# A decoder step on one core: first tiles in halves, a lag on stored tiles, and the last norms paced anew

## The chip, the cores and the metric

The kernel runs on one core of one Trainium2 chip. The metric is the device time of one launch in microseconds. The profile is one such execution, recorded by the hardware; the other times are from executions without a profile.

TensorE (PE in the profile) does the matrix products, VectorE (DVE), ScalarE (ACT) and GpSimd (POOL) work on tiles in on-chip memory, and SyncE (SP) mostly issues transfers. Each engine works through its own instructions in order, and waits where one needs something that another engine or a transfer has not finished.

## The reference

One inference step of a small decoder with two layers, for a prompt of 1024 tokens and 8 decode tokens, all in float32, model width 2048. Cut to what matters here:

```python
def pool_layer(x, ...):                       # layer A
    u, gate = split(x @ w_in)                 # 2048 -> 2 x 2048
    d = multiscale_pool(u)                    # causal means over 2, 4, 8, 16 tokens, minus u
    d = einsum(d, w_grp) * scale              # four groups of 512 x 512
    return layer_norm(ALPHA * x + (d * silu(gate)) @ w_out)

k, v = shared_kv(h)                           # h: output of layer A; 4 heads of 64, rotary on 16

def attn_layer(h, ...):                       # layer B
    q, gate = split(h @ w_in)                 # 32 heads of 64, rotary on 16
    o = attn_core(q, k, v, window=128, sinks)
    return layer_norm(ALPHA * h + (o * silu(gate)) @ w_out)
```

Every layer ends with `layer_norm(ALPHA * x + sub(x))`: the mean and the variance are over the 2048 channels of a token. Outputs are y for prompt and decode tokens, the pooling states, and the last 128 keys and values.

## The kernel before

Channels lie on the 128 partitions, tokens along the free dimension. On-chip memory is cut into 53 slots of 128 x 1040 float32 (`Mem`, names m in the profile), handed out and returned as the work goes. The tokens are two chunks, c = 0 with 512 and c = 1 with 520 (the 8 decode tokens lie behind the prompt's). A pair of channel tiles for one chunk, 128 x (2 x 520), fills a slot.

**Phases.** Four large products follow each other (`PH`): `ai` (input x, weights in_wia), `ao` (input g, weights in_woa, with the residual and layer A's norm), `bi` (input h, weights in_wib and the shared K/V, with attention beside it), `bo` (input o, weights in_wob, the residual and layer B's norm). Each is cut into 2 x 2 blocks and computed with seven block products in place of eight; the seven (idx 0 to 6) run in three groups, A (0 and 5, of chunk 0 alone), C (1, 3, 6) and B (2, 4). For some of them the input is a sum or difference of blocks of both chunks; those are made by `t_ops` and stored in a scratch array (`Td`). `t_gen("x")` makes them for the kernel's input x, one channel pair at a step, with two loads, four VectorE operations and two stores each; the C group of `ai` is the first to read them.

**Units and ticks.** A unit is one block product for one output tile of 128 channels. Each float32 operand is split in two: ScalarE casts the raw tile to a rounded high part (weights L385, inputs L516), VectorE subtracts to get the low part (L393, L522). For each of eight channel tiles three matmuls follow, high x high, high x low, low x high (L589 to L591), so a unit has 24 matmuls of 512 columns in group A, or two halves of 24 matmuls of 260 columns (`HV`). A tick is 12 matmuls of 512 columns or 24 of 260; `self.i` counts ticks. At each one, `end()` issues what stands in a calendar (`on`, `at`, `product`), then the soft tasks that are due or for which a cost model of the engines (`calm`) sees room, then perhaps one step of the first side generator, then up to two loads of inputs (`x_tick`). Side generators (`t_gen`, `ln_gen`) are stepped at least every `every` ticks, provided that `room` slots are free; `pace(n)` sets `every`. The order in which PE, DVE and ACT work is the order in which this program issues instructions; the transfers on SP and GpSimd's work are ordered by a scheduler.

**Loads of inputs.** `x_tick` looks at the next twelve input tiles and issues up to two loads whose sources are written (`x_ready`, by a set `ok` of keys) and for which there is room; `far` is the number of ticks until the tile is read. The input tiles of `ao`, `bi` and `bo` are read back from arrays g, h, o that the kernel itself has written. A key goes into `ok` at the moment that the store is issued. `x_next` picks casts and subtractions of landed tiles; `x_get` forces what a unit needs.

**Start.** `start` issues the first weight tile (512 KB in one transfer), eight x tiles (520 KB each, with two more weights between), then three small arrays of constants: prm, cst, mki. Then come the first weight's split, the splits of four x tiles, the second weight's split, and a cast of a constant matrix, jr, out of cst (L1787). TensorE's first instruction reads the first weight and the first x tile.

**Norms.** Chunk 0 of each of the two norms (`ln_gen` with c = 0, called by `ln0`) runs as a side generator in the B group of `ao` and of `bo`: sums over channels by matmuls with jr, then for eight channel pairs p a subtraction of the mean and a multiplication by 1/sigma on VectorE (L917 to L919), two scalings with per-channel constants on ScalarE (`affine`, L905), and a store on SP (L906). For layer A the result is h, which the `bi` phase reads back (loads at L510); for layer B it is the output y0. Chunk 1 of layer B's norm, output y1, is the last of the kernel. It is done in two token halves of 260 (`HV`): the first half while the last products run (`tail_part` puts its steps on ticks), the second in `tail_end`, behind the last matmul. `tail_sums` (L1265) forms the channel sums by matmul, `tail_stats` copies the mean (L1277), squares it, forms the variance and calls `rstd`, which takes Abs_reciprocal_sqrt on ScalarE and refines it once with three operations (L843 to L845). `tail_norm1` is a subtraction and a multiplication (L1286, L1287), `tail_norm2` two scalings (L1295) and the store. Two of the eight pairs have `tail_norm1` on GpSimd in both halves:

```python
for p in (7, 3):
    self.at(3, lambda p=p: self.tail_norm1(p, h, nc.gpsimd))
for n, p in enumerate((4, 0, 5, 1, 6, 2)):
    self.at(3 + n, lambda p=p: self.tail_norm(p, h))
for n, p in ((6, 7), (8, 3)):
    self.at(n, lambda p=p: self.tail_norm2(p, h))
```

The bank that a product adds to can be seeded by a copy on ScalarE (L711); after a unit its sums are moved out by ScalarE (L615, L649, L658) or VectorE (L660). The attention score products (L1463) and their VectorE partner (L1526) are not touched by the change.

Of the kernel before, what the change touches and what calls it, by code (L numbers as in the profile page):

```python
# [72 lines left out]
X_LOAD, X_CAST, X_LOW, X_FAR, X_SPARE = 9, 4, 3, 22, 8  # L73

# [82 lines left out]
class Kern:  # L157
# [331 lines left out]
    def x_plan(self):  # L489
        self.xl = [(ph, i, j) for ph in PH for _, idxs in GROUPS for i in idxs for j in JS[ph]]  # L490
        self.xraw, self.xhi, self.X = {}, {}, {}
        self.ok = {("x", c, m) for c in range(2) for m in range(NK)}
# [10 lines left out]
    def x_ready(self, k):  # L503
        return all(z in self.ok for z in self.x_src(k)[0])
# [39 lines left out]
    def x_tick(self):  # L544
        free = lambda: len(self.mem.whole())
        n = 0
        for k in self.xl[:12]:
            far = self.x_at(k) - self.i
            if far > X_FAR or n > 1:
                break  # L550
            if self.x_ready(k) and (
                (len(self.xraw) < 4 and free() > X_SPARE + 2) or (far <= X_LOAD and free() > 3) or far <= X_LOAD - 4
            ):
                self.x_load(k)
                n += 1
# [218 lines left out]
    def t_ops(self, A, E, O, Eb, Ob, n, kp, cs=slice(0, TMAX)):  # L774
# [13 lines left out]
        if cs.stop == TMAX:  # L788
            self.ok.add(("t", n, kp))

    def t_gen(self, n):
# [11 lines left out]
        for kp in range(8):  # L803
# [5 lines left out]
            yield  # L809
# [40 lines left out]
    def ln_gen(self, c, pre, acc, gc, bc, out, name):  # L850
# [49 lines left out]
        def affine(p):  # L900
# [6 lines left out]
            if name is not None:  # L907
                self.ok |= {(name, c, 2 * p), (name, c, 2 * p + 1)}
# [88 lines left out]
    def group_unit(self, u):  # L997
# [9 lines left out]
        def post(jj, banks):  # L1007
# [14 lines left out]
            if c == 0:  # L1022
                nc.gpsimd.dma_start(self.act["g", 0][:, m0 : m0 + 2, :TP], t)
                self.ok |= {("g", 0, m0), ("g", 0, m0 + 1)}
# [3 lines left out]
            self.ok.add(("g", 1, m))  # L1028
# [186 lines left out]
    def tail_part(self, q, pos, m, cs):  # L1215
# [54 lines left out]
    def tail_stats(self, h):  # L1270
# [9 lines left out]
        self.rstd(v, r, qq)  # L1280

    def tail_norm1(self, p, h, eng=None):
        eng = eng or self.nc.vector
        b2 = lambda x: x[:, None, h].to_broadcast([P, 2, THM])
        t = self.tv(p)[:, :, h]
        eng.tensor_sub(t, t, b2(self.L["m"]))  # L1286
        eng.tensor_mul(t, t, b2(self.L["r"]))  # L1287
# [10 lines left out]
    def tail_norm(self, p, h):  # L1298
        self.tail_norm1(p, h)
        self.tail_norm2(p, h)  # L1300

    def tail_end(self):
        h = HV[1]
        self.tail_stats(h)
        for p in (2, 7):
            self.tail_norm1(p, h, self.nc.gpsimd)
        for p in (4, 0, 5, 2, 1, 6, 7, 3):
            if p in (2, 7):
                self.tail_norm2(p, h)
            else:  # L1310
                self.tail_norm(p, h)
# [136 lines left out]
    def attend(self, c, t, at):  # L1448
# [103 lines left out]
        def gate():  # L1552
# [7 lines left out]
            if c == 0:  # L1560
                nc.gpsimd.dma_start(self.act["o", 0][:, t, :TP], a.a[:, :TP])
                self.ok.add(("o", 0, t))
# [32 lines left out]
    def o_ok(self):  # L1595
        if self.dec_done:
            for kp in self.half_done:
                self.ok |= {("t", "o", kp), ("o", 1, 2 * kp + 1)}
# [173 lines left out]
    def start(self):  # L1772
        nc, io = self.nc, self.io
        es = [u.ent for u in self.units[:4]]
        es[0]["load"]()
        for n in range(8):
            self.x_load(self.xl[0])
            if n in (3, 5):
                es[n // 2]["load"]()
        nc.sync.dma_start(self.prm[:], io["prm"])  # L1780
        nc.sync.dma_start(self.cst[:], io["cst"])
        nc.sync.dma_start(self.mki[:], io["mki"])
        es[0]["low"]()
        for n in range(4):
            self.x_get(("ai", 0, n))
        es[1]["low"]()
        nc.scalar.copy(self.jr, self.cst[:, K_J : K_J + P])  # L1787
# [23 lines left out]
    def run(self):  # L1811
# [25 lines left out]
        self.on(0, lambda: self.side.append(self.t_gen("x")), 0)  # L1837
# [11 lines left out]
        self.on(f["bo", "B"], pace(2))  # L1849
# [153 lines left out]
```

## Time and profile before

| | before |
|---|---|
| median of 3 runs | 2351.46 us (2350.6 to 2351.57) |
| profiled execution, its own time | 2350.32 us |
| span of the profiled execution | 2348.5 us |
| granted TensorE clock, mean | 0.99 |
| TensorE busy | 2290.5 us, 98% of the span, 16998 matmuls |
| VectorE, ScalarE, GpSimd busy | 66%, 47%, 9% |
| transfers | 555.65 MB, mean 237 GB/s |

The span runs from the first to the last instruction. In rows of the trace the first number is the start in us, the second the busy time of the instruction (or of the group of them), x the number in the group; m is a slot, pD a bank of TensorE's results, and a bracket at the end tells how long the engine had been idle and what ended that. In rows of windows come the stretch, its length, then busy time with the number of instructions for PE, PE's weight loads, DVE, ACT, POOL, the granted clock, the busy share of the transfer engines and GB/s. In the list of waits: engine and operation, what ended the wait, us in total, how many, the longest.

### The profile page before, as it was taken

How to read it: one execution, taken by the hardware profiler on the slowest of the kernel's cores; microseconds unless marked ns; L12 is line 12 of the kernel's file. 1: busy time of each engine (PE TensorE's matmuls, PEld its weight loads, DVE VectorE, ACT ScalarE, POOL GpSimd, SP SyncE). 2: the span in 40 equal slices, each digit the busy share in tenths (PEclk: the TensorE clock that was granted, in tenths of full speed). 3: DMA queues.
4: the chain of work that ended last, by engine and by line, in shares of the span. 5: the costliest groups of instructions: out<-in, count | busy, mean ns of one | idle time of the engine just before them, and what ended most of it. 6: DMA issues, size and time to landing. Idle time of an engine off the chain costs nothing. (4 is left out here: it accounts for less than half of the span.)

```text
span 2348.5 us, 42019 instructions
## 1 busy us (share of the span) xinstructions
PE 2290.5 (98%) x16998; PEld 2132.3 (91%) x16998; DVE 1547.3 (66%) x1840; ACT 1100.6 (47%) x2281; POOL 208.6 (9%) x424
## 2 busy tenths in 40 slices
PE   8999999999999999999999999999999999999994
PEld 6888999999999899988777899999999997799994
DVE  6447756656676686676675866665556676697667
ACT  4334333344243432454665635454656666542455
POOL 1101001100101111000010110100000000111002
PEclk9999999999999999999999999999999999999997
DMA  9858667674748798887596776666644555898844
GB/s 389 289 184 291 212 214 246 222 245 131 265 149 326 241 342 275 299 280 246 166 341 217 250 237 215 213 217 209 214 143 150 165 183 202 273 373 290 281 135 145
DMA packets 194483, 555.65 MB, mean 237 GB/s; under 512 B 31088, under 2 KB 36080, under 8 KB 194288
## 3 DMA queue, kind: packets, MB, share of 16 engines
q1 hardware_dynamic: 152592, 402.42, 52.6%
q0 software_dynamic: 41696, 150.55, 16.4%
q8 instruction: 133, 2.18, 0.4%
q14 instruction: 62, 0.51, 0.1%
HBM read 372.04 MB, written 171.33 MB: 231 GB/s over the span
## 5 line engine op out<-in xcount | busy, mean ns | idle before, releaser
L589 PE MATMUL pD<-m,m 128*128 128x260 f32 (+1 forms) x4800 | 1459.7, 304 | 17.8 <-ACT m L516 7.9
L590 PE MATMUL pD<-m,m 128*128 128x260 f32 (+1 forms) x4800 | 1448.7, 302 | 0.8 <-DVE m L522 0.8
L591 PE MATMUL pD<-m,m 128*128 128x260 f32 (+1 forms) x4800 | 1447.9, 302 | 0.0
L589 PEld LDWEIGHTS pD<-m,m 128*128 128x128 f32 x4800 | 905.8, 189 | 70.7 <-issue 15.6
L590 PEld LDWEIGHTS pD<-m,m 128*128 128x128 f32 x4800 | 906.1, 189 | 36.2 <-DVE m L522 1.9
L591 PEld LDWEIGHTS pD<-m,m 128*128 128x128 f32 x4800 | 905.7, 189 | 35.9
L393 DVE TENSOR_TENSOR m<-m,m 128x1024 fp32r<-128x1024 f32 x366 | 445.0, 1219 | 185.5 <-ACT m L385 169.3
L385 ACT CAST m<-m 128x1024 fp32r<-128x1024 f32 x366 | 381.0, 1045 | 48.8 <-PE pD L590 13.4
L429 DVE TENSOR_TENSOR m<-m,m 128x1024 f32<-128x1024 f32 x200 | 243.8, 1219 | 19.6 <-PE pD L590 7.1
L649 ACT COPY m<-pD 128x260 f32<-128x260 f32 (+1 forms) x126 | 56.0, 445 | 324.3 <-PE pD L591 320.5
L522 DVE TENSOR_TENSOR m<-m,m 128x1040 fp32r<-128x1040 f32 x112 | 134.9, 1235 | 14.6 <-ACT m L516 14.3
L658 ACT ACTIVATE m<-pD 128x260 f32<-128x260 f32 x100 | 38.6, 386 | 202.2 <-PE pD L591 183.2
L516 ACT CAST m<-m 128x1040 fp32r<-128x1040 f32 x112 | 114.5, 1059 | 19.6 <-DVE m L393 6.5
L1526 DVE TENSOR_TENSOR m<-pS,cst 128x1024 f32<-128x1024 f32 x32 | 39.2, 1224 | 120.2 <-ACT m L1525 120.2
L660 DVE TENSOR_TENSOR m<-pD,m 128x260 f32<-128x260 f32 x100 | 42.6, 426 | 113.8 <-PE pD L591 106.4
L1499 ACT ACTIVATE m<-m,sm 128x128 f32<-128x128 f32 x256 | 99.3, 392 | 0.0
L615 ACT ACTIVATE m<-pD 128x512 f32<-128x512 f32 x50 | 29.9, 597 | 137.2 <-PE pD L591 122.7
L1048 PE MATMUL pD<-m,m 128*128 128x260 f32 (+1 forms) x576 | 91.3, 319 | 0.0
L1048 PEld LDWEIGHTS pD<-m,m 128*128 128x128 f32 x576 | 82.0, 188 | 8.2
L1512 ACT ACTIVATE m<-m,sm 128x128 f32<-128x128 f32 x256 | 81.6, 392 | 5.2 <-DVE sm L1507 5.0
L628 ACT ACTIVATE m<-pD 128x260 f32<-128x260 f32 x68 | 26.4, 388 | 117.1 <-PE pD L591 117.0
L630 ACT COPY m<-pD 128x260 f32<-128x260 f32 x68 | 25.6, 376 | 110.5 <-PE pD L591 110.5
(180 smaller groups left out, 1658.7 us busy)
## 6 DMA issues: line engine op xcount, KB each, us to landing
m<-in_wia SPq DMA_DIRECT2D x96, 512.0 KB, 5.3
m<-in_wib SPq DMA_DIRECT2D x96, 512.0 KB, 5.0
m<-in_woa SPq DMA_DIRECT2D x48, 512.0 KB, 6.1
m<-in_wob SPq DMA_DIRECT2D x48, 512.0 KB, 6.2
m<-in_x SPq DMA_DIRECT2D x36, 520.0 KB, 9.8
sbi<-m POOLq DMA_DIRECT2D x36, 512.0 KB, 3.9
m<-sbi SPq DMA_DIRECT2D x36, 512.0 KB, 4.5
sai<-m POOLq DMA_DIRECT2D x32, 512.0 KB, 4.1
```

The costliest lines, as they stand in the source:

```text
L385: self.nc.scalar.copy(e["hi"].r[:, :1024], e["raw"].a[:, :1024])
L393: self.nc.vector.tensor_sub(o.r[:, :1024], s.a[:, :1024], e["hi"].a[:, :1024])
L429: self.nc.vector.tensor_add(s[o].a[:, :1024], s[a].a[:, :1024], s[b].a[:, :1024])
L516: self.nc.scalar.copy(h.r[:, : 2 * TMAX], s.a[:, : 2 * TMAX])
L522: self.nc.vector.tensor_sub(o.r[:, : 2 * TMAX], s.a[:, : 2 * TMAX], h.a[:, : 2 * TMAX])
L589: nc.tensor.matmul(ps[:, :w], wh[:, s], h, start=new and n2 == 0, stop=False, skip_group_check=on)
L590: nc.tensor.matmul(ps[:, :w], wh[:, s], l, start=False, stop=False, skip_group_check=on)
L591: nc.tensor.matmul(ps[:, :w], wl[:, s], h, start=False, stop=n2 == 7, skip_group_check=on)
L649: self.evac(ph, pos)(self.dest(ph, pos, m, 0)(cs), ps[:, : cs.stop - cs.start])
L1048: nc.tensor.matmul(ps[:, : cs.stop - cs.start], ws[:, s], d[:, cs], start=f0 and k == 0, stop=l0 and k == 3,)
L1499: nc.scalar.activation(x["s3"][:, i, :], x["s3"][:, i, :], AF.Exp, bias=nm[:, i : i + 1], scale=0.125, accum_out=rs[:, i : i + 1],)
L1512: nc.scalar.activation(x["s3"][:, i, :], x["s3"][:, i, :], AF.Copy, scale=rs[:, i : i + 1])
```

## The change

It has three parts.

*The start.* The first weight tile and the first x tile are loaded in halves: weight half 0, the two halves of x tile 0, one more x tile, weight half 1, then the others, with the second weight where it was, the third one tile earlier, and the fourth among them too. Each half has a cast and a subtraction of its own. The constants are loaded behind the last x tile, cst first; the cast of jr (and a small VectorE operation on prm) is moved from the start to tick 8. `t_gen("x")` begins at tick 5 in place of 0 and leaves at least four ticks between two channel pairs.

*Loads behind a store.* `ok` keeps the tick at which a key was stored (`landed`). A load that reads g, h or o directly is issued only three ticks later than that (`X_LAG`), as long as its tile is over four ticks away from use (`X_URGE`). Loads from the scratch arrays of sums aren't held back.

*The last norms.* No pair of y1 is on GpSimd. In the first half the eight pairs stand at ticks 3, 4, 4, 5, 5, 6, 6, 7 behind the sums. In `tail_end`, the subtractions of the first two pairs (4 and 0) stand between the Abs_reciprocal_sqrt and the three refining operations, and the eight pairs are in the same order as before. For the side generator of y0's norm `every` is 1 from the start of the B group of `bo` and 2 from 13 ticks later; `room` is 1 from 12 ticks later.

```diff
--- before
+++ after
@@ -71,6 +71,7 @@
 L_LOAD, L_CAST, L_LOW = 11, 6, 4
 SLACK = 1.5
 X_LOAD, X_CAST, X_LOW, X_FAR, X_SPARE = 9, 4, 3, 22, 8
+X_LAG, X_URGE = 3, 4
 
 
 def in_order(tc):
...
@@ -489,7 +490,7 @@
     def x_plan(self):
         self.xl = [(ph, i, j) for ph in PH for _, idxs in GROUPS for i in idxs for j in JS[ph]]
         self.xraw, self.xhi, self.X = {}, {}, {}
-        self.ok = {("x", c, m) for c in range(2) for m in range(NK)}
+        self.ok = {("x", c, m): -99 for c in range(2) for m in range(NK)}
 
     def x_src(self, k):
         ph, i, j = k
...
@@ -500,8 +501,11 @@
         m = 4 * j + o
         return [(n, c, m), (n, c, m + 2)], self.act[n, c][:, m : m + 3 : 2, :]
 
-    def x_ready(self, k):
-        return all(z in self.ok for z in self.x_src(k)[0])
+    def landed(self, *keys):
+        self.ok.update((k, self.i) for k in keys)
+
+    def x_ready(self, k, lag=0):
+        return all(self.ok.get(z, 9999) + lag <= self.i for z in self.x_src(k)[0])
 
     def x_load(self, k):
         self.xl.remove(k)
...
@@ -548,7 +552,7 @@
             far = self.x_at(k) - self.i
             if far > X_FAR or n > 1:
                 break
-            if self.x_ready(k) and (
+            if self.x_ready(k, X_LAG if k[1] not in TROW and far > X_URGE else 0) and (
                 (len(self.xraw) < 4 and free() > X_SPARE + 2) or (far <= X_LOAD and free() > 3) or far <= X_LOAD - 4
             ):
                 self.x_load(k)
...
@@ -806,7 +810,9 @@
             av, bv = a.v(2, TMAX), b.v(2, TMAX)
             self.t_ops(a, av[:, 0], av[:, 1], bv[:, 0], bv[:, 1], n, kp)
             b.free()
-            yield
+            t = self.i + 4
+            while self.i < t:
+                yield
 
 
     def quiet(self):
...
@@ -836,10 +842,11 @@
             yield
         w.free()
 
-    def rstd(self, v, r, q):
+    def rstd(self, v, r, q, between=lambda: None):
 
         nc = self.nc
         nc.scalar.activation(r, v, AF.Abs_reciprocal_sqrt)
+        between()
         nc.vector.tensor_mul(q, r, r)
         nc.vector.scalar_tensor_tensor(q, q, -0.5, v, op0=ALU.mult, op1=ALU.mult)
         nc.vector.scalar_tensor_tensor(r, q, 1.5, r, op0=ALU.add, op1=ALU.mult)
...
@@ -905,7 +912,7 @@
                 nc.scalar.activation(t[:, j], t[:, j], AF.Identity, bias=b, scale=g)
             nc.sync.dma_start(out[:, 2 * p : 2 * p + 2, :T], t)
             if name is not None:
-                self.ok |= {(name, c, 2 * p), (name, c, 2 * p + 1)}
+                self.landed((name, c, 2 * p), (name, c, 2 * p + 1))
 
         for p in range(10):
             load(p + 2)
...
@@ -1244,12 +1251,8 @@
             return
         self.product(1, lambda: self.tail_sums(h, (0, 1), True, True), 1)
         self.at(2, lambda: self.tail_stats(h))
-        for p in (7, 3):
-            self.at(3, lambda p=p: self.tail_norm1(p, h, nc.gpsimd))
-        for n, p in enumerate((4, 0, 5, 1, 6, 2)):
-            self.at(3 + n, lambda p=p: self.tail_norm(p, h))
-        for n, p in ((6, 7), (8, 3)):
-            self.at(n, lambda p=p: self.tail_norm2(p, h))
+        for n, p in zip((3, 4, 4, 5, 5, 6, 6, 7), (4, 0, 5, 1, 6, 2, 7, 3)):
+            self.at(n, lambda p=p: self.tail_norm(p, h))
 
     def tail_sums(self, h, js, first, stop):
 
...
@@ -1277,38 +1280,29 @@
         nc.scalar.copy(m, mb[:, :THM])
         nc.vector.tensor_mul(qq, m, m)
         nc.vector.scalar_tensor_tensor(v, vb[:, :THM], EPS, qq, op0=ALU.add, op1=ALU.subtract)
-        self.rstd(v, r, qq)
-
-    def tail_norm1(self, p, h, eng=None):
-        eng = eng or self.nc.vector
-        b2 = lambda x: x[:, None, h].to_broadcast([P, 2, THM])
+        self.rstd(v, r, qq, between)
+
+    def tail_less(self, p, h):
         t = self.tv(p)[:, :, h]
-        eng.tensor_sub(t, t, b2(self.L["m"]))
-        eng.tensor_mul(t, t, b2(self.L["r"]))
-
-    def tail_norm2(self, p, h):
+        self.nc.vector.tensor_sub(t, t, self.L["m"][:, None, h].to_broadcast([P, 2, THM]))
+
+    def tail_norm(self, p, h, less=True):
         nc = self.nc
+        if less:
+            self.tail_less(p, h)
         t = self.tv(p)[:, :, h]
+        nc.vector.tensor_mul(t, t, self.L["r"][:, None, h].to_broadcast([P, 2, THM]))
         for j in range(2):
             m = 2 * p + j
             g, b = (self.prm[:, i + m : i + m + 1] for i in (C_GB, C_BB))
             nc.scalar.activation(t[:, j], t[:, j], AF.Identity, bias=b, scale=g)
         nc.sync.dma_start(self.io["y1"][:, 2 * p : 2 * p + 2, h], t)
 
-    def tail_norm(self, p, h):
-        self.tail_norm1(p, h)
-        self.tail_norm2(p, h)
-
     def tail_end(self):
         h = HV[1]
-        self.tail_stats(h)
-        for p in (2, 7):
-            self.tail_norm1(p, h, self.nc.gpsimd)
+        self.tail_stats(h, lambda: [self.tail_less(p, h) for p in (4, 0)])
         for p in (4, 0, 5, 2, 1, 6, 7, 3):
-            if p in (2, 7):
-                self.tail_norm2(p, h)
-            else:
-                self.tail_norm(p, h)
+            self.tail_norm(p, h, p not in (4, 0))
 
 
     def partner(self, s, n, T):
...
@@ -1772,22 +1766,49 @@
     def start(self):
         nc, io = self.nc, self.io
         es = [u.ent for u in self.units[:4]]
-        es[0]["load"]()
-        for n in range(8):
+        e, k = es[0], self.xl.pop(0)
+        raw, x = self.mem.full(), self.mem.full()
+        half = [slice(512 * i, 512 * i + 512) for i in range(2)]
+        xs = [slice(TMAX * i, TMAX * i + TMAX) for i in range(2)]
+        src = self.x_src(k)[1]
+        w = self.quads("ai", 0)[0]
+        nc.sync.dma_start(raw.a[:, half[0]], w[:, half[0]])
+        for i in range(2):
+            nc.sync.dma_start(x.a[:, xs[i]], src[:, i, :])
+        for n in range(7):
             self.x_load(self.xl[0])
-            if n in (3, 5):
-                es[n // 2]["load"]()
+            if n == 0:
+                nc.sync.dma_start(raw.a[:, half[1]], w[:, half[1]])
+            elif n in (2, 3, 5):
+                es[(n + 1) // 2]["load"]()
+        nc.sync.dma_start(self.cst[:], io["cst"])
         nc.sync.dma_start(self.prm[:], io["prm"])
-        nc.sync.dma_start(self.cst[:], io["cst"])
         nc.sync.dma_start(self.mki[:], io["mki"])
-        es[0]["low"]()
-        for n in range(4):
+        hi, lo, xh, xo = (self.mem.full() for _ in range(4))
+        def split(s, h, o, c):
+            nc.scalar.copy(h.r[:, c], s.a[:, c])
+            nc.vector.tensor_sub(o.r[:, c], s.a[:, c], h.a[:, c])
+
+        split(raw, hi, lo, half[0])
+        for i in range(2):
+            split(x, xh, xo, xs[i])
+        self.x_get(("ai", 0, 1))
+        split(raw, hi, lo, half[1])
+        e.update({"hi": hi, "lo": lo, "in": True, "did": {"cast", "low"}})
+        self.X[k] = xh, xo
+        for s in (raw, x):
+            s.free()
+        for n in range(2, 4):
             self.x_get(("ai", 0, n))
         es[1]["low"]()
-        nc.scalar.copy(self.jr, self.cst[:, K_J : K_J + P])
-        nc.vector.tensor_scalar(
-            self.nsink[:], self.prm[:, C_SINK : C_SINK + NH], -1.0, None, op0=ALU.mult
-        )
+
+        def consts():
+            nc.scalar.copy(self.jr, self.cst[:, K_J : K_J + P])
+            nc.vector.tensor_scalar(
+                self.nsink[:], self.prm[:, C_SINK : C_SINK + NH], -1.0, None, op0=ALU.mult
+            )
+
+        self.on(8, consts)
         z = self.mem.full()
         nc.gpsimd.memset(z.a[:, :144], 0.0)
 
...
@@ -1834,7 +1855,7 @@
         def ln1():
             self.side.append(self.ln_gen(1, {}, self.acc, C_GA, C_BA, self.act["h", 1], "h"))
 
-        self.on(0, lambda: self.side.append(self.t_gen("x")), 0)
+        self.on(5, lambda: self.side.append(self.t_gen("x")), 0)
         for g in range(2):
             t = f["ai", "B"] + 40 * g
             for k in (g, g + 2):
...
@@ -1846,7 +1867,9 @@
         self.on(f["bi", "A"], pace(2))
         self.on(f["bi", "A"] + 1, ln1)
         self.on(f["bo", "B"] + 3, lambda: ln0("bo", C_GB, C_BB, io["y0"], None))
-        self.on(f["bo", "B"], pace(2))
+        self.on(f["bo", "B"], pace(1))
+        self.on(f["bo", "B"] + 13, pace(2))
+        self.on(f["bo", "B"] + 12, lambda: setattr(self, "room", 1))
         self.on(f["bo", "B"], self.tail_open, 0)
         self.use_four(True)
         self.on(f["bi", "A"], lambda: self.use_four(False), 0)
```

The other hunks put `self.landed(...)` in the place of `self.ok.add(...)` and `self.ok |= {...}`, and an argument `between` through `tail_stats`.

More of the change, by code (lines that the diff above doesn't have):

```diff
@@ L788, in t_ops @@
         if cs.stop == TMAX:
-            self.ok.add(("t", n, kp))
+            self.landed(("t", n, kp))
     def t_gen(self, n):
@@ L1023, in post @@
                 nc.gpsimd.dma_start(self.act["g", 0][:, m0 : m0 + 2, :TP], t)
-                self.ok |= {("g", 0, m0), ("g", 0, m0 + 1)}
+                self.landed(("g", 0, m0), ("g", 0, m0 + 1))
                 G.free(True)
@@ L1027, in post @@
             nc.gpsimd.dma_start(self.act["g", 1][:, m, :], t[:, 1])
-            self.ok.add(("g", 1, m))
+            self.landed(("g", 1, m))
             def sums():
@@ L1268, in tail_sums, with tail_stats @@
                 )
-    def tail_stats(self, h):
+    def tail_stats(self, h, between=lambda: None):
         nc = self.nc
@@ L1561, in gate @@
                 nc.gpsimd.dma_start(self.act["o", 0][:, t, :TP], a.a[:, :TP])
-                self.ok.add(("o", 0, t))
+                self.landed(("o", 0, t))
                 self.ao.pop((c, t)).free(True)
@@ L1597, in o_ok @@
             for kp in self.half_done:
-                self.ok |= {("t", "o", kp), ("o", 1, 2 * kp + 1)}
+                self.landed(("t", "o", kp), ("o", 1, 2 * kp + 1))
     def gate_done(self, c, t0, s):
```

## The prediction

> **What bounds the kernel now.** I read the page first, then TensorE's own waits, then the order of time at the places that these name.
>
> ```profile
> span 2348.5 us, 42019 instructions
> ...
> PE 2290.5 (98%) x16998; PEld 2132.3 (91%) x16998; DVE 1547.3 (66%) x1840; ACT 1100.6 (47%) x2281; POOL 208.6 (9%) x424
> ```
> ```profile
> PE pS L1463 <- DVE m L1526: 8.8, 4, 3.9
> PE pD L589 <- ACT m L516: 7.9, 1, 7.9
> PE pD L589 <- ACT pD L711: 7.8, 3, 5.1
> PE pD L589 <- ACT m L658: 1.2, 1, 1.2
> ```
>
> TensorE is the bound: it is busy for 98% of the span, and the change leaves the number and the order of its matmuls as they are. So only three things can move the time: when the first matmul starts, the few stalls between, and what follows the last matmul. The waits list the stalls (us in total, times, longest). The first, 7.9, is the wait for the first tile; of the 7.8 behind L711, one wait of 5.1 is most. The 8.8 behind L1526 lie in attention, which the change does not touch.
>
> **The start.**
>
> ```profile
> 5.16 1.04 ACT L385 CAST m<-m 128x1024 fp32r<-128x1024 f32 x1 [3.14 <-DMA m<-in_wia]
> ...
> 6.76 1.06 ACT L516 CAST m<-m 128x1040 fp32r<-128x1040 f32 x1 [0.56 <-DMA m<-in_x]
> ...
> 7.85 5.31 DVE L522 TENSOR_TENSOR m<-m,m 128x1040 fp32r<-128x1040 f32 x4 [0.39 <-ACT m L516]
> 7.87 0.79 PE L589 MATMUL pD<-m,m 128*128 128x512 f32 x1 [7.87 <-ACT m L516]
> ...
> 10.82 1.06 ACT L516 CAST m<-m 128x1040 fp32r<-128x1040 f32 x1 [0.28 <-DMA m<-in_x]
> ...
> 13.15 0.63 PE L590 MATMUL pD<-m,m 128*128 128x512 f32 x1
> ...
> 13.58 0.50 PE L591 MATMUL pD<-m,m 128*128 128x512 f32 x1
> ...
> 13.92 0.39 PE L589 MATMUL pD<-m,m 128*128 128x512 f32 x1
> ...
> 16.69 0.40 PE L589 MATMUL pD<-m,m 128*128 128x512 f32 x1
> ...
> 19.68 0.30 ACT L1787 CAST jr<-cst 128x128 fp32r<-128x128 f32 x1 [6.54 <-DMA cst<-in_cst]
> ...
> 23.40 0.50 PE L589 MATMUL pD<-m,m 128*128 128x512 f32 x1 [0.97 <-ACT m L615]
> ```
> ```profile
> L982 ACT CAST m<-m 128x512 fp32r<-128x512 f32 x3 | 1.9, 620 | 0.9 <-DVE m L966 0.9
> ...
> L983 DVE TENSOR_TENSOR m<-m,m 128x512 fp32r<-128x512 f32 x3 | 2.1, 690 | 3.3 <-ACT m L982 3.3
> ```
>
> The weight tile lands at 5.16, the first x tile at 6.76, the fourth at 10.82: (10.82 - 6.76) / 3 = 1.35 us for each. The new order asks for the halves that the first matmul needs ahead of the rest. Half a tile takes about 0.67, so the first weight half lands at 5.16 - 0.67 = 4.5 and the first x half at 5.15; with a half cast of 0.62 the first matmul starts at 5.8 in place of 7.87. The splitting adds two casts and two subtractions of 0.62 and 0.69, which lie in time in which both engines waited for data (the idle time in the brackets).
>
> This doesn't carry through in full. The bytes ahead of the fourth x tile are the same, so it lands at 10.82 as before; the cast (1.06) and the subtraction (four in 5.31, ending at 13.16) make it whole at 13.15. The first unit has 24 matmuls, and the 20th is the first to read that low part: 13.15 + 5 x 0.23 = 14.3 is the earliest end. The other limit is the rate: 13.15 to 13.58 is one matmul per 0.43 us, 13.92 to 16.69 is twelve at 0.23, so TensorE ran at half rate from 7.87 to 13.6, 5.7 us. The same 5.7 after 5.8 is 11.5; twelve matmuls are done by then and twelve at 0.23 follow: 14.4. Before, the second unit began at 16.69. Gain 2.3. The Trainium skill (TensorE: Matmul & The Clock Gate, "What's actually happening") speaks against part of this: the rate is set by free-running windows of some 3.4 us, so an early start may only buy more matmuls at half rate. By it the gain here is an estimated 1.7 to 2.4; its late end is a rival below.
>
> The third unit began at 23.40, though 16.69 + 24 x 0.23 = 22.2. The brackets tell why: ScalarE sat for 6.54 until 19.68 before the cast of jr, which waits for the constants, and the weight and x casts and the eviction L615 stood behind it. The change moves that cast to tick 8 and issues the constants behind the last x tile; the x tiles and weights have then landed by 20.3 (six more at 1.35 behind 12.2), and nothing in the first units reads the constants. Gain 1.2. The transforms of x begin five ticks later, 14 us, and each takes at least four ticks; eight of them end long before the C group, 72 ticks in, so I cost this at nothing. Start: 3.5, bounds 1.5 (a half transfer that lands no sooner, and the jr gain) and 4.0.
>
> **The norm of h and its loads.**
>
> ```profile
> 1032.05 0.36 SPq L906 DMA_DIRECT2D h<-m  x1
> ...
> 1040.62 1.03 SPq L510 DMA_DIRECT2D m<-h  x2
> ...
> 1045.11 1.06 ACT L516 CAST m<-m 128x1040 fp32r<-128x1040 f32 x1 [5.73 <-DMA m<-h]
> ...
> 1049.29 0.59 PE L589 MATMUL pD<-m,m 128*128 128x260 f32 x1 [5.09 <-ACT pD L711]
> ```
> ```profile
> 2324.17 4.32 ACT L905 ACTIVATE m<-m,prm 128x512 f32<-128x512 f32 x6
> ```
> ```profile
> 1049.20:1054.90 5.70, 5.62 (x26) 5.62 (x27) 2.64 (x3) 2.72 (x6) 0.00 (x0) 0.50 0.90 321
> 1054.90:1060.60 5.70, 5.70 (x49) 5.70 (x49) 2.71 (x3) 5.37 (x8) 0.00 (x0) 1.00 0.96 346
> ```
>
> SP issues the store of h at 1032.05 and stands until 1040.62 before the load that reads it; the tile lands at 1045.11; ScalarE, in order, waits 5.73 with its cast; the copy into the accumulator (L711) stands behind, and TensorE waits 5.09. The third fence shows the aftermath: at a granted clock of 0.50, 26 matmuls in 5.70, and 49 in the next 5.70. So 26 x (5.70 / 26 - 5.70 / 49) = 2.7 are lost beside the 5.1: 7.8 are at stake.
>
> With the lag these loads are asked for three ticks after the store, and in the built order two more affine pairs stand ahead of the first pair of h casts. The load still waits for its store on SP, with later stores and a weight load behind it, and I see no reason for it to land before 1045.1. But ScalarE reaches that cast later: to the 1039.4 at which it ran dry come two affine pairs (the second fence has six of these affines, later in the run, at 0.72 each: 2.9) and two small copies, an estimated 1 with the handing over: 3.9, so some 1.8 of the wait is left. That is too little to halve the clock: the stretch quoted next has waits of 2.2 and 1.2 and a granted clock of 1.00. I take 7.8 - 1.8 = 6.0, bounds 2.0 (it waits nearly as long for the next pair) and 7.8.
>
> **The last stretch.**
>
> ```profile
> 2300.00:2322.00 22.00, 17.35 (x123) 15.45 (x122) 21.29 (x27) 13.11 (x25) 2.53 (x2) 1.00 0.46 165
> ```
> ```profile
> 2303.12 1.10 ACT L1295 ACTIVATE m<-m,prm 128x260 f32<-128x260 f32 x2 [5.35 <-DVE m L1287]
> ...
> 2305.95 0.39 PE L589 MATMUL pD<-m,m 128*128 128x260 f32 x1 [2.16 <-ACT pD L711]
> ...
> 2320.86 1.16 PE L1265 MATMUL pD<-m,cst 128*128 128x260 f32 x4 [0.93 <-DVE m L660]
> ...
> 2325.71 1.23 DVE L919 TENSOR_TENSOR m<-m,m 128x1024 f32<-128x1024 f32 x1
> ...
> 2328.40 0.35 ACT L1277 COPY m<-pD 128x260 f32<-128x260 f32 x1
> ...
> 2330.70 1.39 DVE L844 SCALAR_TENSOR_TENSOR m<-m 128x260 f32<-128x260 f32 x1
> ...
> 2332.12 0.43 DVE L845 SCALAR_TENSOR_TENSOR m<-m,m 128x260 f32<-128x260 f32 x1
> ...
> 2333.20 1.66 DVE L1287 TENSOR_TENSOR m<-m,m 128x520 f32<-128x520 f32 x1
> ...
> 2334.78 1.77 DVE L1286 TENSOR_TENSOR m<-m,m 128x520 f32<-128x520 f32 x1
> ...
> 2336.59 0.70 DVE L1287 TENSOR_TENSOR m<-m,m 128x520 f32<-128x520 f32 x1
> ...
> 2337.20 0.69 DVE L1286 TENSOR_TENSOR m<-m,m 128x520 f32<-128x520 f32 x1
> ...
> 2338.67 6.04 ACT L1295 ACTIVATE m<-m,prm 128x260 f32<-128x260 f32 x12 [0.25 <-DVE m L1287]
> ...
> 2341.97 0.70 DVE L1287 TENSOR_TENSOR m<-m,m 128x520 f32<-128x520 f32 x1
> ```
>
> VectorE is busy for 21.29 of 22.0, so ScalarE waits for it, and TensorE for ScalarE: 2.2 here and the 1.2 behind L658. The change takes three steps of y0's norm out of this stretch (two operations like L919's 1.23 each, 7.4 in all) and GpSimd's contention, and adds two tiles to VectorE ((2341.97 - 2336.59) / 4 = 1.35 each, 2.7): it falls to about 15. The seeding copy now stands ahead of most affines. The steps go to the time before 2300, where VectorE has room: the mean is 66%, a step is 2.45 in two ticks of 2.9. I take 2.5 of the 3.4, bounds 0 and 3.4.
>
> **Behind the last matmul** (the same fence). TensorE ends at 2320.86 + 1.16 = 2322.0, but the statistics start at 2328.40, behind the rest of y0's norm (the six affines from 2324.17, shown with h). In the changed program's order nothing of y0 stands there: they start at about 2322.1. Gain 6.3.
>
> From 2328.40 to the last affine (2338.67 + 6.04 = 2344.7) are 16.3. New count: copy, square and variance 1.3 (0.35, and 0.45 each by L845); two subtractions 1.4 (L1287's 0.70 each; in part of it VectorE waited for the root); three refining steps 1.3 at 0.43, since L844's 1.39 against L845's 0.43 goes with GpSimd; two multiplies 1.4 (L1286); six tiles at 1.35, 8.1; the last two affines 1.0 (6.04 / 12 each): 14.5. The two tiles that GpSimd had cost 2.7 more on VectorE, and 0.96 + 0.96 + 1.08 of stretched operations (L844, L1287, L1286) go. Gain 1.8; the last store and the end, 3.8, stay. Sum 8.1, bounds 7 and 8.6.
>
> **The rivals.** *The wait on h moves along:* the next pair, which needs stores that SP issues behind the waiting load, stalls instead. For it: SP's wait (1032.05 to 1040.62) stays in the order. The gain there is 2: 2335.4.
>
> *The clock keeps its own time:* half rate ends at an edge that does not move with the first matmul. The trace's one start, 5.7 us of it, can't tell. If the edge comes 1.1 later than forecast, at 12.6, (12.6 - 5.8) / 0.43 = 15.8 matmuls are begun, 15 are done, and the unit ends at 12.6 + 9 x 0.23 and a little: 15.0. That is 0.6 less: 2332.0. The Trainium skill's rule quoted with the start (TensorE: Matmul & The Clock Gate) is what would make the edge so, by its windows at an estimated 3.4 to 6.8 us behind the first matmul.
>
> *The end stays as it is:* the new pace doesn't finish y0's norm in time on the chip, and 6.3 and 2.5 go: 2340.2. Against it: the order is fixed at build time.
>
> *Slower: the lag starves the phases.* Every first-chunk load of g, h and o may come three ticks late, 3 x 2.9 = 8.7 (24 matmuls in 5.70 / 49 x 24 = 2.8 and a little); if TensorE waits for that at the start of three phases, 26 are lost and the 6 as well: 2363.4. It decides from 20 us of new waits. Against it: the lag is dropped within four ticks of need, and ScalarE's order differs at h alone. For it: the loads are issued in another order by SP throughout, and the trace of before can't show what that does.
>
> **How the numbers follow.** 3.5 + 6.0 + 2.5 + 8.1 = 20.1. The profiled execution took 2350.3 for its span of 2348.5 and becomes 2330.2; the runs' median, 1.1 above it, becomes 2331.4. Chances: forecast 0.62, wait moves 0.15, clock 0.08, end 0.04, slower 0.11. All upper bounds give 23.8, 2327.7, and the untouched attention stalls can go either way by a microsecond or two: 2326. All lower ones give 10.5, 2341.0; I stop at 2340, which leaves out the slower rival and the third at its worst. The gain can vanish only by the slower rival: of its 0.11 I give 0.02 to an end within 0.2% (4.7 us, about what a measurement can tell) and 0.09 to slower; faster is 0.89.
>
> **What would show it.** Right: first matmul near 5.8, third unit near 20; no TensorE wait over 2 and no clock of 0.50 around 1040; the copy of the mean within 0.3 of the last matmul, no GpSimd in the norm, 14.5 from there to the last affine. Wrong: an SP wait on h that still ends in a ScalarE wait of 4 or more; TensorE waits behind L715 or L662 from 2230 on; new waits for x casts at a phase's start.

## The result and the profile after

| | before | after |
|---|---|---|
| median | 2351.16 us (2350.6 to 2351.57) | 2325.91 us (2324.88 to 2327.5) |
| ratio, 95% interval | | 0.9893 (0.9876 to 0.9911) |
| profiled execution, its own time | 2350.32 us | 2326.44 us |
| its span, granted clock | 2348.5 us, 0.990 | 2324.5 us, 0.993 |

The changed kernel is faster by 25.2 us between the medians and by 23.9 between the two profiled executions, where 20.1 was forecast. The median lies 0.1 under the lower end of the range (2326.0). First the page of the changed kernel and TensorE's waits in it (us in total, times, longest); line numbers are up to 7 higher or 6 lower than before, outside of the new start.

```profile
PE 2286.2 (98%) x16998; PEld 2129.5 (92%) x16998; DVE 1546.7 (67%) x1850; ACT 1100.9 (47%) x2283; POOL 195.6 (8%) x416
```
```profile
PE pS L1457 <- DVE m L1520: 10.1, 5, 4.8
PE pD L593 <- ACT m L1789: 5.9, 1, 5.9
...
PE pD L594 <- DVE m L526: 0.6, 1, 0.6
PE pD L593 <- ACT pD L715: 0.6, 1, 0.6
```

Of 7.8 us behind the copy into the accumulator (L711, now L715) 0.6 is left, and the first wait is 5.9 in place of 7.9. Of the waits over 1 us only those in attention (L1463, now L1457) are no shorter: 4.8 at the longest against 3.9. The order of time, at the start:

```profile
4.54 1.93 ACT L1789 CAST m<-m 128x512 fp32r<-128x512 f32 x3 [2.53 <-DMA m<-in_wia]
...
5.87 0.80 PE L593 MATMUL pD<-m,m 128*128 128x512 f32 x1 [5.87 <-ACT m L1789]
...
11.99 0.50 PE L594 MATMUL pD<-m,m 128*128 128x512 f32 x1 [0.59 <-DVE m L526]
...
14.64 0.40 PE L593 MATMUL pD<-m,m 128*128 128x512 f32 x1
...
20.21 0.40 PE L593 MATMUL pD<-m,m 128*128 128x512 f32 x1
```

First matmul 5.87 (forecast 5.8), second unit 14.64 (14.4), third unit 20.21 (near 20). At the norm of h, ScalarE and then SP:

```profile
1033.91 1.53 ACT L912 ACTIVATE m<-m,prm 128x512 f32<-128x512 f32 x2 [1.11 <-DVE m L926]
...
1036.59 2.03 ACT L520 CAST m<-m 128x1040 fp32r<-128x1040 f32 x2
1038.93 0.38 ACT L715 COPY pD<-m 128x260 f32<-128x260 f32 x1 [0.31 <-DVE m L664]
1039.24 1.52 ACT L912 ACTIVATE m<-m,prm 128x512 f32<-128x512 f32 x2
1041.06 0.39 ACT L662 ACTIVATE m<-pD 128x260 f32<-128x260 f32 x1 [0.30 <-PE pD L595]
1041.35 1.04 ACT L386 CAST m<-m 128x1024 fp32r<-128x1024 f32 x1
1042.28 1.06 ACT L520 CAST m<-m 128x1040 fp32r<-128x1040 f32 x1
```
```profile
1037.56 0.56 SPq L371 DMA_DIRECT2D m<-in_wkv  x1
1043.87 0.36 SPq L514 DMA_DIRECT2D m<-h  x1
```

The casts of h (L520) have no bracket: ScalarE no longer waits for one here. SP still stands, from 1038.1 (1037.56 + 0.56) to 1043.9. In before it issued a weight load behind the store of 1032.05:

```profile
1035.47 0.35 SPq L370 DMA_DIRECT2D m<-in_wkv  x1
```

So it stood there from 1035.8 to 1040.6, for 4.8 us, and for 5.8 now. The end, with VectorE's and ScalarE's last operations, and the window of the 22 us before the last matmul's end:

```profile
2306.02 1.04 PE L1268 MATMUL pD<-m,cst 128*128 128x260 f32 x4
```
```profile
2306.66 0.38 ACT L1280 COPY m<-pD 128x260 f32<-128x260 f32 x1 [2.03 <-PE pD L1268]
...
2320.03 1.10 ACT L1298 ACTIVATE m<-m,prm 128x260 f32<-128x260 f32 x2 [0.30 <-DVE m L1294]
```
```profile
2307.60 0.43 DVE L1282 SCALAR_TENSOR_TENSOR m<-pD,m 128x260 f32<-128x260 f32 x1
2307.95 1.30 DVE L1287 TENSOR_TENSOR m<-m,m 128x520 f32<-128x520 f32 x2
2309.17 0.42 DVE L850 TENSOR_TENSOR m<-m 128x260 f32<-128x260 f32 x1
2309.62 0.43 DVE L851 SCALAR_TENSOR_TENSOR m<-m 128x260 f32<-128x260 f32 x1
```
```profile
2285.00:2307.00 22.00, 21.55 (x166) 20.59 (x164) 17.65 (x31) 14.64 (x31) 0.00 (x0) 1.00 0.35 122
```

The copy of the mean follows the last matmuls at once, VectorE goes through variance, two subtractions and the refining without a pause, and from the copy to the last affine it is 2320.03 + 1.10 - 2306.66 = 14.5. Before the end TensorE works for 21.55 of 22 us, where it was 17.35.

### The profile page after: what moved, and what is told of

Its sections match the earlier page's. It is cut to its first block, busy times and chain, and to the rows that moved or that the text cites. A ratio compares the mean times of both kernels' runs of the same rounds, so it can differ in the third digit from the quotient of the medians.

```text
span 2324.5 us, 42005 instructions
## 1 busy us (share of the span) xinstructions
PE 2286.2 (98%) x16998; PEld 2129.5 (92%) x16998; DVE 1546.7 (67%) x1850; ACT 1100.9 (47%) x2283; POOL 195.6 (8%) x416
## 5 line engine op out<-in xcount | busy, mean ns | idle before, releaser
L386 ACT CAST m<-m 128x1024 fp32r<-128x1024 f32 x365 | 380.0, 1044 | 50.8 <-PE pD L594 13.3
L520 ACT CAST m<-m 128x1040 fp32r<-128x1040 f32 x111 | 113.4, 1060 | 21.7 <-DVE m L394 9.3
L1520 DVE TENSOR_TENSOR m<-pS,cst 128x1024 f32<-128x1024 f32 x32 | 39.2, 1224 | 121.3 <-ACT m L1519 121.2
L962 DVE TENSOR_TENSOR m<-m 128x512 f32<-128x512 f32 (+5 forms) x80 | 55.7, 697 | 34.5 <-ACT m L953 21.0
```

The costliest lines, as they stand in the source:

```text
L386: self.nc.scalar.copy(e["hi"].r[:, :1024], e["raw"].a[:, :1024])
L520: self.nc.scalar.copy(h.r[:, : 2 * TMAX], s.a[:, : 2 * TMAX])
```

## The experiments

**One part at a time.** Each part of the change was put alone on the kernel before, with its edit as in the change:

```diff
# p_start
+        nc.sync.dma_start(raw.a[:, half[0]], w[:, half[0]])
...
+        self.on(8, consts)
...
+        self.on(5, lambda: self.side.append(self.t_gen("x")), 0)
# p_lag
+            if self.x_ready(k, X_LAG if k[1] not in TROW and far > X_URGE else 0) and (
# p_tail
+        self.on(f["bo", "B"], pace(1))
...
+        for n, p in zip((3, 4, 4, 5, 5, 6, 6, 7), (4, 0, 5, 1, 6, 2, 7, 3)):
...
+        self.tail_stats(h, lambda: [self.tail_less(p, h) for p in (4, 0)])
```

> The kernel before with the start's part alone (halves, constants late, jr at tick 8, the transforms of x from tick 5). If the three parts add, it ends 3.5 to 4.0 us under before (ratio 0.9984), and the profile keeps the wait of 5 us near 1046, the waits near 2302 and the 6 us behind the last matmul. If the early start only pays because something later in the change uses it, the gain has shrunk to under 1 us by 1000 us.

> The kernel before with the lag of three ticks alone. If it is the lag that takes the wait on h away, the stall near 1049 and the half clock behind it go: 7 to 8 us under before (ratio 0.9968), nothing else moves. If the wait moves along to the next pair, 2 us. If it was the shift of the start that removed it, nothing is gained here.

> The kernel before with the last norms' part alone. If the parts add: 13 to 13.6 us under before (ratio 0.9943), 9 of them behind the last matmul and 4 to 4.5 in waits between 2250 and 2322. If the last stretch's stalls need the other parts, 9 us.

| part alone | ratio to before | interval | median |
|---|---|---|---|
| start | 0.9985 | 0.9976 to 0.9993 | 2346.95 us |
| lag | 0.9966 | 0.9953 to 0.9978 | 2343.36 us |
| last norms | 0.9951 | 0.9939 to 0.9964 | 2338.2 us |

The product of the three is 0.9902, inside the interval of the whole change: the parts add. The start's gain does not fade on the way either: in its trace the fourth unit is 3.3 us ahead of before, and the last matmul 3.6 (2.6 at its least in between, leaving out the stalls themselves). With the lag alone, matmul 7,368 (near 1050) starts 7.9 us ahead; this is the wait and the half clock behind it. There ScalarE reaches the cast that had waited without a wait:

```profile
1044.47 1.04 ACT L386 CAST m<-m 128x1024 fp32r<-128x1024 f32 x1
1045.41 1.06 ACT L520 CAST m<-m 128x1040 fp32r<-128x1040 f32 x1
```

That trace ends only 4.8 ahead, since attention's stall, described below, took 6.6 us in it and 3.9 in before; the medians differ by 7.3. The last norms alone end the trace 13.6 us earlier, 8.9 of them behind the last matmul.

**ScalarE's order, or the loads?** The loads of h stay at their tick here; only their casts are allowed later:

```diff
-            if due <= self.i or (t + 3 <= self.i and free > X_SPARE and len(self.xhi) < 2):
+            if due <= self.i or (t + (6 if k[0] == "bi" and k[1] in (0, 5) else 3) <= self.i and free > X_SPARE and len(self.xhi) < 2):
```

> The kernel before; only the casts of h's first-chunk tiles are asked for six ticks behind their load in place of three, so two or three more affine pairs stand ahead of them in ScalarE's order, and the loads on SP stay nearly where they are. Theory one: the order on ScalarE causes the stall, and a late load is harmless to TensorE as long as no ScalarE work that it needs stands behind its cast; then the stall of 5.1 and the half clock go here too, 7 to 8 us under before, without any lag of the loads. Theory two: the lag helps since the loads no longer stand on SP in front of later stores; then SP still waits for the store here, the next pairs come late, and 2 us or less is gained.

Ratio 0.9968 (0.9956 to 0.998), the same as with the lag, and matmul 7,368 starts 7.7 us ahead. TensorE's waits, and SP in order of time:

```profile
PE pS L1463 <- DVE m L1526: 9.2, 5, 4.5
PE pD L589 <- ACT m L516: 8.0, 1, 8.0
PE pD L589 <- ACT pD L711: 2.7, 2, 2.2
```
```profile
1032.75 3.24 SPq L906 DMA_DIRECT2D h<-m  x2
1041.61 1.12 SPq L510 DMA_DIRECT2D m<-h  x2
```

The wait of 5.1 behind L711 is gone, though SP issues the load as late as ever (1041.61 against 1040.62 before). Theory one holds: what a late load costs is decided by what stands behind its cast in ScalarE's order.

**The end: pace or GpSimd?** One kernel has the new pace alone on the kernel before, the other takes the pace out of the changed kernel:

```diff
# t_pace (on before)
-        self.on(f["bo", "B"], pace(2))
+        self.on(f["bo", "B"], pace(1))
+        self.on(f["bo", "B"] + 13, pace(2))
+        self.on(f["bo", "B"] + 12, lambda: setattr(self, "room", 1))
# t_norm (on after): the same three lines back to one
```

> The kernel before with the new pace of y0's norm alone (every tick from the B group of bo on, room 1); y1's halves stay as they were, two pairs of each on GpSimd. If the pace is what frees the end, the mean's copy follows the last matmul at once (6.4 to 6.8 us), and most of the 4.5 us of waits before it go too, since three steps of the norm leave the last 20 us: 10 to 11 us under before (ratio 0.9955). If GpSimd's share is what starves TensorE there, 7 us, and the waits of 2.2 and 1.2 stay.

> The changed kernel with the pace of before (every two ticks, room 4); y1's halves without GpSimd and with the two subtractions ahead. If the pace frees the end, 9 to 10 us over the changed kernel: the last matmul is late by 3 or more, and some 6 us of y0's norm stand ahead of the mean's copy again. If the end was freed by the tiles' new ticks, 2 us or less over it. Against before: ratio 0.9933 by the first, 0.990 by the second.

Ratios to before 0.9951 (0.9935 to 0.9966) and 0.993 (0.9916 to 0.9944). ScalarE's last rows, first of the pace alone, then of the changed kernel without it:

```profile
2316.56 0.35 ACT L1277 COPY m<-pD 128x260 f32<-128x260 f32 x1
...
2326.81 6.05 ACT L1295 ACTIVATE m<-m,prm 128x260 f32<-128x260 f32 x12 [0.24 <-DVE m L1287]
```
```profile
2315.42 1.52 ACT L912 ACTIVATE m<-m,prm 128x512 f32<-128x512 f32 x2 [0.88 <-DVE m L926]
2316.84 0.35 ACT L1280 COPY m<-pD 128x260 f32<-128x260 f32 x1
...
2330.18 1.10 ACT L1298 ACTIVATE m<-m,prm 128x260 f32<-128x260 f32 x2 [0.31 <-DVE m L1294]
```

The two do different things. With the pace alone it is still 2326.81 + 6.05 - 2316.56 = 16.3 from copy to last affine, as before; with the whole third part alone it is 14.5. Without the pace, TensorE has new waits of 2.4 and 1.8 and y0's affines (L912) stand ahead of the copy: the trace is 10.2 longer than that of the changed kernel. With the pace alone on before, the trace is 11.9 shorter; 4.3 of it lie in the last 20 us before the last matmul and 6.1 behind it, and 1.2 come from the half clock near 1050, which lasted 3.4 us there in place of 6.8. So the pace is worth some 10 in either kernel, and the norms' new form the rest of 13.6, some 3. The times without a profile can't show that rest: the pace alone and the whole third part alone both have a ratio of 0.9951. Whether GpSimd's absence or the two subtractions ahead make the 1.8 inside wasn't tried apart. The rows have a part for each: an operation that took 1.39 beside GpSimd (L844) takes 0.43 in after (L851), and the subtractions fill the 0.5 us for which VectorE waited for the root in before:

```profile
2330.24 0.43 DVE L843 TENSOR_TENSOR m<-m 128x260 f32<-128x260 f32 x1 [0.49 <-ACT m L842]
```

**The same again, and the start's pieces.** The changed kernel beside the others, and then with one piece of the start undone at a time:

```diff
# a_jr
-        self.on(8, consts)
+        consts()
# a_whole
-        nc.sync.dma_start(raw.a[:, half[0]], w[:, half[0]])
+        nc.sync.dma_start(raw.a[:, :1024], w)
...
# a_tgen
-            t = self.i + 4
-            while self.i < t:
-                yield
+            yield
...
-        self.on(5, lambda: self.side.append(self.t_gen("x")), 0)
+        self.on(0, lambda: self.side.append(self.t_gen("x")), 0)
```

> The changed kernel once more, beside which the other runs of this call stand: ratio to before 0.988 to 0.991. The half rate at the start ends 3.4 to 6.8 us behind the first matmul, at another point than the 4.09 of the first profile if it keeps a grid of its own; again at 4.1 if it is tied to the first matmul.

> The changed kernel with the cast of jr back among the first casts (the constants are still loaded last). If ScalarE's place in the order is what held up the third unit, it is late again, by more than the 1.2 us of before, since the constants land later than before: third unit at 22 or later in place of 20.2. If the constants' transfer was the point, nothing changes.

> The changed kernel with the first weight tile and the first x tile in one transfer and one cast each. The first matmul is back at 7.8 in place of 5.8. By the forecast the second unit begins 2.3 later, at 16.9. If the fourth x tile and not the first sets the first unit's end, under 1 later: 14.7 to 15.6, and the halves are worth that little.

> The changed kernel with the transforms of x from tick 0 on and a step at each chance, as before. The forecast cost the delay at nothing: the fourth unit begins within 0.3 of 25.8, and the time is within 1.5 us. If their 32 loads and stores crowd the first units' weights, the units before 60 us begin 1 us late or more.

The changed kernel again: 0.9887 (0.9874 to 0.9901). With jr back among the first casts, 2335.08 us in one execution; ScalarE and TensorE there, and the window behind:

```profile
21.12 0.30 ACT L1806 CAST jr<-cst 128x128 fp32r<-128x128 f32 x1 [7.63 <-DMA cst<-in_cst]
```
```profile
24.83 0.79 PE L593 MATMUL pD<-m,m 128*128 128x512 f32 x1 [4.25 <-ACT m L619]
```
```profile
22.93:29.76 6.83, 4.93 (x12) 3.87 (x13) 6.83 (x7) 6.13 (x8) 1.34 (x3) 0.50 1.02 410
```

The third unit is 4.6 late, and the half clock that follows makes it 7.0 by the fourth (32.74 against 25.79). Loading the constants last is only harmless because the cast is out of the way. With whole tiles (2326.31 us in one execution) the first matmul is at 7.90 again, the second unit at 16.28 in place of 14.64: 1.6, between the two expectations. The same 1.6 at the third and fourth units isn't all kept: 1.1 is left by 838 us, and the span is that of the changed kernel (2324.49 against 2324.53), after stalls in attention that happened to differ. What the halves bring at the end is thus not settled. Without the delay of the transforms the fourth unit is 0.4 late and 0.1 is left by 878; of the 3.6 by which this one execution ended later, more than the 1.5 expected, 3.2 came at the attention stall (7.5 us of it in place of 4.8) and the half clock behind it. At the start, costing the delay at nothing stands; that the longer stall has nothing to do with it is not shown by one execution, though the same stall took 3.8 in the changed kernel's repetition.

**The stall in attention.** It is the largest left: 3.9 us near 1244 in the first profile of before, 3.8 to 7.5 in the executions since that kept this place as it was. In the changed kernel:

```profile
1229.12 2.36 DVE L1321 TENSOR_TENSOR m<-m,m 128x1024 f32<-128x1024 f32 x2 [6.01 <-DMA m<-m]
1231.52 1.22 DVE L1428 TENSOR_TENSOR m<-m,m 128x1024 f32<-128x1024 f32 x1
1232.66 1.22 DVE L1520 TENSOR_TENSOR m<-pS,cst 128x1024 f32<-128x1024 f32 x1
...
1233.93 0.80 PE L1457 MATMUL pS<-m,m 64*128 64x256 f32 x2 [4.75 <-DVE m L1520]
```
```profile
1200.00:1231.90 31.90, 29.12 (x160) 22.88 (x158) 21.19 (x28) 16.83 (x40) 7.53 (x16) 1.00 1.00 340
1231.94:1238.76 6.82, 4.83 (x19) 3.46 (x20) 3.18 (x4) 1.00 (x2) 0.00 (x0) 0.50 0.97 333
```

VectorE waits 6.01 for the partner tile of q's rotation with the product that TensorE needs (L1520) behind it: the same pattern as h's. Two remedies, the order and the transfers:

```diff
# b_r1: rotation of tiles 2, 4, 6 one tick later
-        self.soft("v", self.i + 3, self.i + (4 if t0 > 7 or not c else 7), b)
+        n2 = 1 if t0 > 0 and t0 < 8 and not c else 0
+        self.soft("v", self.i + 3 + n2, self.i + n2 + (4 if t0 > 7 or not c else 7), b)
# b_far: loads of h's transforms later
             if far > X_FAR or n > 1:
                 break
+            if k[0] == "bi" and k[1] in TROW and far > 12:
+                break
```

> The changed kernel, and the rotation of q for the first chunk's tiles 2, 4 and 6 is put one tick later on VectorE, so that the product with the mask stands ahead of it (the same remedy as for h's casts: nothing that TensorE needs stands behind an operation that waits for a transfer). If VectorE's order causes the stall of 3.9 to 7 us near 1235, the stall and the half clock behind it go: 5 to 8 us under the changed kernel, ratio to before 0.986 to 0.987. If the scores need the rotated tile itself, the stall moves to the next score product, and nothing or 1 us is gained.

> The changed kernel; the loads of h's transformed tiles (th) are issued at most 12 ticks ahead of their use in place of 22, so three of them no longer stand in front of q's partner transfers near 1216. If the stall of 3.9 to 7 us near 1235 is a crowd of transfers (busy share 0.92 to 1.04 from 1200 to 1235), the partner tiles land in 6 us in place of 10.7, stall and half clock go: 4 to 8 us under the changed kernel, ratio to before 0.986 to 0.987. If the stores of the norm set that rate, the stall stays: 0.989. If 12 ticks are too few, new waits for th casts come behind 1290, and it is slower.

The order is the wrong remedy here: 0.9937 (0.9924 to 0.9949), some 12 us over the repetition of the changed kernel, against my theory. Its waits:

```profile
PE pS L1458 <- DVE m L1428: 11.1, 3, 3.7
```

The score product needs the rotated tile itself, so each of the three moved tiles pays 3.7 where one tile paid before. Easing the transfers works: 0.9854 (0.9837 to 0.987), 2316.29 us, 8.9 under the repetition of the changed kernel (2325.19 us), whose interval of ratios lies above this one. Before was 1.4 lower when it was measured beside this kernel, so by the ratios the gain is some 7.8. It is faster than both kernels. The rotation, and the same two stretches:

```profile
1225.00 2.36 DVE L1323 TENSOR_TENSOR m<-m,m 128x1024 f32<-128x1024 f32 x2 [0.84 <-DMA m<-m]
```
```profile
1200.00:1231.90 31.90, 31.79 (x179) 25.21 (x178) 24.39 (x30) 17.90 (x41) 8.06 (x19) 1.00 0.95 340
1231.94:1238.76 6.82, 6.82 (x55) 5.32 (x52) 4.66 (x6) 4.84 (x13) 0.36 (x1) 1.00 0.46 156
```

The wait for the partner is 0.84, TensorE has no gap and no half clock, and the busy share of the transfer engines is 0.46 behind it in place of 0.97. Ahead of it the share is hardly lower, 0.95 in place of 1.00; what differs is what stands in front. In the changed kernel SP issues three loads of th between 1212.5 and 1215.5, and the four partner transfers right behind them land 10.1 to 11.3 us after their issue. Without the three they land after 4.9 to 5.8, and VectorE's order up to the rotation is the same in both traces. It was a crowd of transfers, and three of the tiles in it were not needed yet. Of the 6.7 us by which this trace is shorter than the repetition's, 5.1 lie at this stall. Another 2.1 lie near 1940, where the next wait is 1.9 in place of 3.2 and no half clock follows; whether the edit does that too is not shown.

## Why the prediction was right, and where it was off

| term | forecast | measured, profiled executions |
|---|---|---|
| start, to the fourth unit | 3.5 | 3.7 |
| wait on h and half clock | 6.0 | 7.8 |
| stalls before the last matmul | 2.5 | 4.5 |
| behind the last matmul | 8.1 | 9.0 |

The measured column is how much further the changed kernel's trace is ahead behind each place than in front of it, matmul by matmul. These are 25.0; the stretches between them take back 1.0, most of it at attention's stall (4.8 us in this execution, 3.9 before) and ahead of the norm of h, which makes the 24.0 of the spans. All four terms had the right sign and mechanism, and all were too small: the first within its bounds, the second at its upper one (7.8), the last two past theirs (3.4 and 8.6). Together they put the median 0.1 past the end of the range.

*Start.* The half transfers and half casts did what the sum said. The second unit's start of 14.64 against 14.4 is close for a partly wrong reason: I carried over 5.7 us of half rate. In the 14 traces the full rate begins between 3.34 and 6.89 us behind the first matmul, 4.09 in the changed kernel and 3.48 in its repetition. The fixed 5.7 is refuted. By the Trainium skill (TensorE: Matmul & The Clock Gate, "What's actually happening") the rate is set in free-running windows of some 3.4 us, which makes the lag an estimated 3.4 to 6.8; the measured 3.34 to 6.89 agree to within 0.1. In the changed kernel TensorE then waited 0.59 at 11.99 for the third x tile's low part, so the earlier clock bought little. The rival of a late edge took no part.

*The wait on h.* The step that was mis-sized is "some 1.8 of the wait is left". I gave ScalarE the busy time of two affine pairs and two copies, 3.9, on its way to the cast. With the lag alone on before, it reaches that cast at 1045.41, 6.0 behind the 1039.4 where it had run dry, and the tile landed at 1045.11 in before. About half of the missing 2.1 is a weight cast that also moved ahead of it and that the sum left out (L386, 1.04 in the rows above, right ahead of the last cast); the rest is ScalarE's own short waits for VectorE and TensorE, which the brackets show. The rival in which the wait moves to the next pair did not happen. That SP would go on waiting was right, and harmless, though the forecast had it standing from 1032.05 and overlooked the weight load at 1035.47.

*The last stretch.* The forecast took 2.5 of 3.4. It left out the waits ahead of L1265, 0.93 of which stood in the very row that I quoted for the last matmul, and it doubted the rest. The repaced kernel keeps 0.5 there (2.2, 1.2, 0.9 and 0.4 before). VectorE is busy for 17.65 of 22, not for 15: the matmuls of those 22 us are 166 in place of 123, so more of the surrounding work falls into them.

*Behind the last matmul.* Statistics at once, 14.5 inside: both as forecast (6.3 and 1.8; the sum swaps the names of L1286 and L1287, which take the same 0.69 and 0.70). The rest is counting. I took the copy to follow the end of the last matmul, but in after it starts with it (2306.66 against 2306.68), so 6.8 go in place of 6.3. The time from the last affine to the end went from 3.8 to 3.4, where I had left it as it was.

*Slower, or not as said.* No new waits for casts came at the start of a phase; the longest new wait of TensorE for ScalarE is 0.3.

## What to carry to other kernels

An operation that waits for a transfer costs what stands behind it on its engine, not what the transfer takes; find the first instruction behind it that TensorE needs. If nothing needs the waiting operation soon, put it later in the order (h's casts, 7 us); if TensorE needs its result, bring its transfer forward (q's rotation, 12 us lost by the one and some 8 won by the other). Work off the end of a program by letting the side work in front of it run early: ten of the 25 us here came from three lines that set a pace.

## What the runs showed of the hardware

The same wait costs different amounts. A wait of 5.1 in before and one of 4.9 with the pace alone, at the same place, were followed by 6.8 and by 3.4 us of half clock. The wait of 2.2 ahead of the last matmuls halved the clock for 3.4 us in the traces of the start alone and of the lag alone, and not at all in before and with the casts later; the forecast's "too little to halve the clock" was thus no rule. The lag of full rate behind the first matmul spread over 3.34 to 6.89, with the smaller values (3.34 to 4.23) all in kernels whose first matmul came before 6.1, and the larger (4.38 to 6.89) all in those that began at 7.8 or later. Why these two groups differ is open. Every stretch of half clock between this first rise and the last matmul, in all 14 traces, lasted 3.41, 6.83 or 10.24 us, that is one, two or three times 3.41: a wait's price in clock came in steps.
